# A dilated 3x3 convolution: the last input pair loaded in eighteen transfers instead of one

## The chip, the cores and the metric

The kernel runs on one core of a Trainium2 chip. Five engines take part: TensorE (PE; its weight loads are shown apart as PEld), VectorE (DVE), ScalarE (ACT), GpSimd (POOL) and SyncE (SP), with 16 DMA engines behind the DMA queues. The metric is the device time of one execution in microseconds, as a median of runs. The profile takes one execution apart; its times count from the start of its span.

## The reference

The input holds 16 images of 64 channels, 64 rows and 64 columns, the weights are 128 x 64 x 3 x 3, and the dilation is 2. Each output pixel is a sum over input channels and nine taps that lie two pixels apart, with zeros around the image; all is float32.

```
x_pad = np.pad(x, ((0, 0), (0, 0), (pad, pad), (pad, pad)), mode='constant')
...
output[b, co] += weight[co, ci, kh, kw] * x_pad[b, ci, kh*dilation:kh*dilation+h, kw*dilation:kw*dilation+w]
```

## The kernel before

**Pairs.** Two images of 64 channels fill the 128 partitions, so there are NP = 8 pairs. TensorE works through pair 0 to pair 7. It uses the lower 64 partitions for one image and the upper 64 for the other, with matmuls of the two alternating. Each pair has NU = 4 parts (u = 0 to 3) of 16 rows.

**Arithmetic.** Rows are taken in groups of four, two even ones (e = 0) and two odd ones (e = 1). For the middle tap the kernel first adds the two halves of each group on GpSimd (`prepare`, L127, into s16), convolves that sum once (the "w1" phase), copies the result out of PSUM on ScalarE (L189), and then, for each half, convolves the inputs with differences of weights ("w21", "w01") and with the outer taps, and adds the copied part on VectorE (L194) into the output tile o. So a pair needs both its input x16 and its sums s16.

**Loads.** `load` (L69 to L72) takes a new x16 tile, one of six buffers, and issues from GpSimd's queue a DMA which reads float32 from memory and writes float16 into the tile. Pair 0 is loaded in two transfers, by rows, and pairs 1 to 4 in one each, all at the start. In the loop, at u = 1 of pair pb, the load of pair pb + 2 is put on the queue (L180, L181), for pairs 5, 6 and 7, followed by the first part of the sums of pair pb + 1 (L184) and, at u = 2, by the second (L186). GpSimd takes these in program order, and it runs ahead of TensorE as far as buffers allow: s16 has three buffers, so the sums of pair n wait until TensorE has finished pair n - 3.

**Semaphores.** The completions of the loads on GpSimd's queue go round eight semaphores. In the kernel before there are nine loads, and only the ninth uses a semaphore again, the first one.

**Outputs.** SP issues the output DMAs (L205) when VectorE has filled a tile: two halves of 1 MB in each of two steps for pairs 0 and 7, and two of 2 MB for the others, 20 in all. The output tiles have three buffers.

**Order around the change.** On GpSimd's queue the load of pair 7 comes after the sums of pair 5 and before those of pair 6, which come before those of pair 7. On TensorE, pair 7 first needs its sums (L172 from s16), and then its input (L172 from x16).

Of the kernel before, what the change touches and what calls it, by code (L numbers as in the profile page):

```python
# [10 lines left out]
def kernel(  # L11
# [7 lines left out]
    nc = tc.nc  # L19

    B, CI, H, W = x.shape
# [5 lines left out]
    P = 128  # L27
    f32 = mybir.dt.float32
    f16 = mybir.dt.float16
    NP = B // 2  # L30
# [19 lines left out]
    x16pool = ctx.enter_context(tc.tile_pool(name="x16pool", bufs=6))  # L50
# [8 lines left out]
    x_pair = x.rearrange("(nb two) c h w -> nb (two c) h w", two=2)  # L59
# [5 lines left out]
    x16 = {}  # L65
# [3 lines left out]
    def load(pb, cuts):  # L69
        x16[pb] = x16pool.tile([P, H, W], f16, tag="x16", name=f"x16_{pb}")  # L70
        for lo, hi in zip(cuts, cuts[1:]):
            nc.gpsimd.dma_start(out=x16[pb][:, lo:hi], in_=x_pair[pb, :, lo:hi])  # L72

    cuts0 = [0, 20, 36, 52, H]
    AHEAD = 5
    load(0, [0, 36, H])
    load(1, [0, H])


# [14 lines left out]
    for name, a in (("w21", 2), ("w01", 0)):  # L94
        for u in range(2):
            nc.vector.tensor_sub(  # L96
                out=w16[:, SLOT[name] * KW : (SLOT[name] + 1) * KW, u, :],
# [5 lines left out]
    for n, name in enumerate(("w1", "w21", "w0", "w01", "w2")):  # L103
        ps = cpool.tile([P, 2, NB], f32, tag="ps", name=f"wt{n}")
        k0 = SLOT[name] * KW
        for j in range(KW):
            nc.tensor.matmul(  # L107
                out=ps[:, 0, j * CO : (j + 1) * CO],
# [12 lines left out]
    def prepare(pb, lo, hi):  # L121
        if pb not in s16:
            s16[pb] = sumpool.tile([P, 2 * NQ, W], f16, tag="s16", name=f"s16_{pb}")
        src = x16[pb].rearrange("p (q e r) w -> p q e (r w)", e=2, r=2)
        dst = s16[pb].rearrange("p (q r) w -> p q (r w)", r=2)
        q0, q1 = lo // 4, hi // 4
        nc.gpsimd.tensor_add(  # L127
            out=dst[:, q0:q1], in0=src[:, q0:q1, 0, :], in1=src[:, q0:q1, 1, :]
        )

    prepare(0, 0, 20)
    for pb in range(2, AHEAD):
        load(pb, [0, H])
# [33 lines left out]
    def phase(pb, u, terms):  # L167

        ps = cpool.tile([CO, 2, NB], f32, tag="ps", name="ps")
        for pair in zip(*(conv(pb, hb, ps[:, hb], u, terms) for hb in range(2))):  # L170
            for m in pair:
                nc.tensor.matmul(**m)  # L172
        return ps

    for pb in range(NP):
        o = opool.tile([P, 2, H, W], f32, tag="o", name=f"o{pb}")
        ov = o.rearrange("p b (q e r) w -> p b q e (r w)", e=2, r=2)
        for u in range(NU):

            if u == 1 and AHEAD <= pb + 2 < NP:  # L180
                load(pb + 2, [0, H])  # L181
            if pb + 1 < NP:
                if u == 1:
                    prepare(pb + 1, 0, 36)  # L184
                elif u == 2:
                    prepare(pb + 1, 36, H)  # L186

            s32 = spool.tile([P, 2, NB], f32, tag="s32", name="s32")
            nc.scalar.copy(out=s32, in_=phase(pb, u, [("w1", 2, 0)]))  # L189
            for e, terms in enumerate(  # L190
                ([("w21", 1, 0), ("w0", 1, -1)], [("w01", 0, 0), ("w2", 0, 1)])
            ):
                ps = phase(pb, u, terms)
                nc.vector.tensor_add(  # L194
                    out=ov[:, :, u * UQ : (u + 1) * UQ, e, :],
                    in0=ps.rearrange("p b (q c) -> p b q c", c=QW),
                    in1=s32.rearrange("p b (q c) -> p b q c", c=QW),
                )


            step = NU // 2 if pb in (0, NP - 1) else NU
            if (u + 1) % step == 0:
                fl = slice((u + 1 - step) * 4 * UQ, (u + 1) * 4 * UQ)
                for hb in range(2):
                    nc.sync.dma_start(out=out[2 * pb + hb, :, fl], in_=o[:, hb, fl])  # L205
# [35 lines left out]
```

## Time and profile before

| What | Value |
|---|---|
| Median of 3 runs | 128.02 us (127.53 to 128.8) |
| Profiled execution, its own time | 127.64 us |
| Its span | 125.9 us |
| Granted TensorE clock, mean | 0.956 |
| Matmuls of L172 on x16 | 768, 86.6 us busy |
| Sums on POOL (L127) | 18, 34.0 us busy |
| Loads on POOL's queue (L72) | 9 issues, 570 ns each; to landing 7.1 to 22.8 us |
| Outputs on SP's queue (L205) | 20 issues; to landing 9.1 to 24.9 us |
| Read from and written to memory | 17.07 MB and 33.55 MB |

A page of the profile gives each engine's busy time, then the span in 40 equal slices (a digit is the busy share in tenths), then the DMA queues (q0 is GpSimd's, software_dynamic; q1 is SP's, hardware_dynamic) with the share of the time of 16 DMA engines that their packets took, and the chain of work that ended last. The DMA view gives the same rows of DMA for any stretch of time, with slices of that stretch. A timeline gives an engine's instructions in order: start, duration, line and operation, what it writes and reads, and, in brackets, how long the engine was idle before and what ended that.

### The profile page before, as it was taken

Reading aid. Unit: us, or ns where it says so; the run is one execution under the profiler, and the core shown is the slowest. Engines: PE = TensorE matmul, PEld = TensorE weight load, DVE = VectorE, ACT = ScalarE, POOL = GpSimd, SP = SyncE. Lnnn points to the kernel's source line nnn. Section 1 sums busy time; section 2 is a strip of 40 time slices with the busy share of each in tenths; the row PEclk is TensorE's granted clock in tenths of the full one; section 3 lists DMA queues with packets and bytes.
Section 4 is the critical chain, followed back from the end, with each engine's and each line's share of the span. In section 5 each row is a group of like instructions: output and inputs, shape, how many; then the busy total and the mean of one; then the engine's idle time right before and its main releaser. Section 6 shows DMA issues by size and latency. Waiting matters only on the chain.

```text
span 125.9 us, 2253 instructions
## 1 busy us (share of the span) xinstructions
PE 106.6 (85%) x981; PEld 54.7 (43%) x981; DVE 80.7 (64%) x72; ACT 37.0 (29%) x37; POOL 39.6 (31%) x33
## 2 busy tenths in 40 slices
PE   6348999999999999999999999999999999950000
PEld 2143455555555555555555555555555555520000
DVE  0550367787778777877778778777877787770000
ACT  4733033333333333333333333333333333310000
POOL 6139797868077008600840093000000000000000
PEclk9999999999999999999999999999999999997555
DMA  4899999999999999999999999999999999999981
GB/s 107 143 215 223 213 211 216 234 281 294 401 292 284 383 297 323 328 427 312 312 325 419 427 432 432 437 417 417 437 427 458 417 409 417 437 411 427 427 349 47
DMA packets 4329, 42.37 MB, mean 337 GB/s; under 512 B 480, under 2 KB 480, under 8 KB 864
## 3 DMA queue, kind: packets, MB, share of 16 engines
q1 hardware_dynamic: 3024, 33.85, 63.8%
q0 software_dynamic: 1296, 8.39, 32.9%
q8 instruction: 7, 0.11, 0.3%
q14 instruction: 2, 0.02, 0.0%
HBM read 17.07 MB, written 33.55 MB: 402 GB/s over the span
## 4 chain that ended last, share of the span: by engine, by line
PE 80%; DMA 6%; POOL 1%; DVE 1%; DVEq 1%; issue 1%; POOLq 0%
PE ps L172 80%; DMA x<-in_x_dram 6%; POOL s L127 1%; DVE o L194 1%; DVEq L236 1%; DVEq L194 0%; POOLq L222 0%
## 5 line engine op out<-in xcount | busy, mean ns | idle before, releaser
L194 DVE TENSOR_TENSOR o<-ps,s 128x1024 f32<-128x1024 f32 x64 | 77.0, 1223 | 27.9 <-PE ps L172 26.2
L172 PE MATMUL ps<-x,w_sb 64*128 64x496 f16 (+3 forms) x768 | 86.6, 372 | 0.0
L172 PEld LDWEIGHTS <-w_sb 64*128 64x128 f16 x960 | 52.5, 96 | 51.5 <-issue 5.2
L189 ACT COPY s<-ps 128x1024 f32<-128x1024 f32 x32 | 32.4, 1012 | 70.3 <-PE ps L172 70.3
L127 POOL TENSOR_TENSOR s<-x 128x1152 f16<-128x1152 f16 (+4 forms) x18 | 34.0, 1911 | 36.1 <-PE ps L172 27.8
L172 PE MATMUL ps<-s,w_sb 64*128 64x496 f16 (+1 forms) x192 | 26.5, 379 | 2.1 <-POOL s L127 2.1
L72 POOL DMA_DIRECT2D x<-in_x_dram x9 | 5.1, 570 | 0.8 <-POOLq L222 0.8
L87 PE MATMUL warm<-zero 128*128 128x512 f16 x6 | 2.7, 627 | 1.2 <-DVE zero L81 1.2
L107 PE MATMUL wt<-ident,w 128*128 128x128 f16 x15 | 1.8, 312 | 2.0 <-ACT w L93 2.0
L96 DVE TENSOR_TENSOR w<-w 128x192 f16<-128x192 f32 x4 | 1.7, 495 | 2.5 <-DMA w<-in_weight_dram 2.5
L107 PEld LDWEIGHTS <-w 128*128 128x128 f16 x15 | 1.5, 145 | 2.9 <-ACT w L93 2.9
L93 ACT CAST w<-w 128x576 f16<-128x576 f32 x2 | 2.3, 1212 | 1.6 <-DMA w<-in_weight_dram 1.6
L116 DVE CAST w_sb<-wt 128x384 f16<-128x384 f32 x3 | 1.7, 557 | 1.4 <-PE wt L107 1.2
L87 PEld LDWEIGHTS <-zero 128*128 128x128 f16 x6 | 0.7, 135 | 2.3 <-DVE zero L81 1.2
L93 ACT ACT_TABLE_LOAD x1 | 1.3, 1283 | 0.7 <-PEq L222 0.7
L118 ACT CAST w_sb<-wt 128x384 f16<-128x384 f32 x2 | 1.0, 479 | 1.1 <-PE wt L107 1.1
L81 DVE MEMSET zero<- 128x256 uint32 x1 | 0.3, 272 | 0.9 <-PEq L222 0.9
masks.py:199 POOL TENSOR_SCALAR_AFFINE_SELECT ident<-ident 128x128 f16<-128x128 f16 x1 | 0.3, 295 | 0.1
masks.py:197 POOL MEMSET ident<- 128x128 f16 x1 | 0.2, 233 | 0.0
L222 POOL MEMSET const-float32-0.0<- 128x1 f32 x1 | 0.1, 100 | 0.2 <-issue 0.2
L222 POOL MEMSET const-bfloat16-1.0<- 128x1 bf16 x1 | 0.1, 103 | 0.0
L222 POOL MEMSET const-uint8-127<- 128x1 uint8 x1 | 0.1, 103 | 0.0
(1 smaller groups left out, 0.1 us busy)
## 6 DMA issues: line engine op xcount, KB each, us to landing
out_dram<-o SPq DMA_DIRECT2D x12, 2048.0 KB, 16.8
out_dram<-o SPq DMA_DIRECT2D x8, 1024.0 KB, 12.3
x<-in_x_dram POOLq DMA_DIRECT2D x7, 1024.0 KB, 15.5
x<-in_x_dram POOLq DMA_DIRECT2D x1, 576.0 KB, 7.1
x<-in_x_dram POOLq DMA_DIRECT2D x1, 448.0 KB, 8.6
w<-in_weight_dram SPq DMA_DIRECT2D x1, 288.0 KB, 2.8
```

What stands on the lines that cost most here:

```text
L72: nc.gpsimd.dma_start(out=x16[pb][:, lo:hi], in_=x_pair[pb, :, lo:hi])
L87: nc.tensor.matmul(out=warm[:, 0], lhsT=zero[:, 0:P], rhs=zero, start=True, stop=True)
L93: nc.scalar.copy(out=w16[:, 0:NK, u, :], in_=w32k)
L96: nc.vector.tensor_sub(out=w16[:, SLOT[name] * KW : (SLOT[name] + 1) * KW, u, :], in0=w32k[:, a * KW : (a + 1) * KW, :], in1=w32k[:, KW : ...
L107: nc.tensor.matmul(out=ps[:, 0, j * CO : (j + 1) * CO], lhsT=w16[:, k0 + j, :, :].rearrange("o t i -> o (t i)"), rhs=ident, start=True, st ...
L116: nc.vector.tensor_copy(out=dst, in_=ps[:, 0, 0 : KW * CO])
L118: nc.scalar.copy(out=dst, in_=ps[:, 0, 0 : KW * CO])
L127: nc.gpsimd.tensor_add(out=dst[:, q0:q1], in0=src[:, q0:q1, 0, :], in1=src[:, q0:q1, 1, :])
L172: nc.tensor.matmul(**m)
L189: nc.scalar.copy(out=s32, in_=phase(pb, u, [("w1", 2, 0)]))
L194: nc.vector.tensor_add(out=ov[:, :, u * UQ : (u + 1) * UQ, e, :], in0=ps.rearrange("p b (q c) -> p b q c", c=QW), in1=s32.rearrange("p b ( ...
L236: with _tile.TileContext(nc) as tc:
```

## The change

Pair 7, the last, is no longer loaded by one transfer of 128 partitions with 64 rows, but by 18 transfers, all from GpSimd's queue, at the same place in the program. Partitions 112 to 127 are taken two at a time, eight times: first the rows from 0 to 2, 4, 6 ... 16, another number for each two partitions, and then, in a second round, the rest of their first 20 rows (18, 16, 14 ... 4 rows). Then come rows 20 to 64 of these 16 partitions in one transfer, and at last all rows of partitions 0 to 111 in one. All else stays. As the eight semaphores are used again, GpSimd waits, from the eighth transfer on, for the transfer eight places before (for the eighth, that is the load of pair 6); and TensorE and the sums of pair 7 wait for eight semaphores where they waited for one.

```
+    TWOS = range(P - 16, P, 2)
+    TOP = 20
+
+    def load_twos(pb):
+        x16[pb] = x16pool.tile([P, H, W], f16, tag="x16", name=f"x16_{pb}")
+
+        def part(p0, p1, lo, hi):
+            nc.gpsimd.dma_start(
+                out=x16[pb][p0:p1, lo:hi], in_=x_pair[pb, p0:p1, lo:hi]
+            )
+
+        for n, p in enumerate(TWOS):
+            part(p, p + 2, 0, 2 * n + 2)
+        for n, p in enumerate(TWOS):
+            part(p, p + 2, 2 * n + 2, TOP)
+        part(P - 16, P, TOP, H)
+        part(0, P - 16, 0, H)
...
             if u == 1 and AHEAD <= pb + 2 < NP:
-                load(pb + 2, [0, H])
+                if pb + 2 < NP - 1:
+                    load(pb + 2, [0, H])
+                else:
+                    load_twos(pb + 2)
```

## The prediction

> **What bounds the kernel now.** First I read the page: the row of DMA shares, the queues, and the chain that ended last.
>
> ```profile
> span 125.9 us, 2253 instructions
> ...
> PE 106.6 (85%) x981; PEld 54.7 (43%) x981; DVE 80.7 (64%) x72; ACT 37.0 (29%) x37; POOL 39.6 (31%) x33
> ...
> DMA  4899999999999999999999999999999999999981
> ...
> DMA packets 4329, 42.37 MB, mean 337 GB/s; under 512 B 480, under 2 KB 480, under 8 KB 864
> ...
> q1 hardware_dynamic: 3024, 33.85, 63.8%
> q0 software_dynamic: 1296, 8.39, 32.9%
> ...
> PE 80%; DMA 6%; POOL 1%; DVE 1%; DVEq 1%; issue 1%; POOLq 0%
> ```
>
> The chain names TensorE, but its last piece ends at 113.3 us, 12.6 us before the span does, and the DMA row is at 9 from the third slice nearly to the end. So I asked the DMA view for the stretch after the last load and for the last 6 us.
>
> ```profile
> DMA packets 1771, 22.58 MB, mean 426 GB/s; under 512 B 203, under 2 KB 203, under 8 KB 203
> ...
> q1 hardware_dynamic: 1764, 22.51, 100.0%
> ```
>
> That is 67 to 120 us: the output queue alone fills all 16 DMA engines. The next is 120 to 126 us, in 40 slices of 0.15 us:
>
> ```profile
> DMA  9999999999967671615131312120000000000000
> ```
>
> The engines run dry one after another. The landing records of the last output (sixteen completions, one per engine) run from 121.9 to 124.8 us, with their mean at 123.0. So the end is set by the DMA engine that has most work, not by TensorE: the last two outputs are issued at 113.3 and 113.7 us, and the latest engine comes to them at 119.9 (124.8 less two 1 MB outputs of 2.45 us each, the spacing of the landings at the end). TensorE, VectorE and SP could be about 6 us late before that engine lacked work; only what is added to an engine's packets, or a delay beyond that cover, reaches the end.
>
> Then POOL's timeline, since the change is on its queue:
>
> ```profile
> 51.98 0.57 POOL L72 DMA_DIRECT2D x<-in_x_dram  x1
> 60.20 4.21 POOL L127 TENSOR_TENSOR s<-x 128x1152 f16<-128x1152 f16 x2 [7.65 <-PE ps L172]
> 72.55 4.21 POOL L127 TENSOR_TENSOR s<-x 128x1152 f16<-128x1152 f16 x2 [8.15 <-PE ps L172]
> ```
>
> The first line is the issue of pair 7's load, then the sums of pairs 6 and 7, each waiting for TensorE. POOL does nothing after 76.8. Who needs these? TensorE's timeline:
>
> ```profile
> 96.35 0.81 PE L172 MATMUL ps<-s,w_sb 64*128 64x512 f16 x6
> 96.98 2.55 PE L172 MATMUL ps<-x,w_sb 64*128 64x512 f16 x24
> ```
>
> At 96.35 pair 7 begins with its sums; at 96.98 it reads its input. In time of need the load has 40 us of cover.
>
> **The change part by part.**
>
> *Bytes.* The same elements are loaded once each: 112 full partitions, 16 partitions by 44 rows, and 16 by 20 rows in sixteen pieces. Change in bytes: 0.
>
> *Issues on POOL.* One issue becomes 18. The row of L72 has 0.53 to 0.69 us each; 17 x 0.57 = 9.7 us more on POOL. Behind them stand the sums of pair 6 and then of pair 7.
>
> *New waits on POOL.* Completion semaphores of POOL's loads go round eight, so the eighth small transfer waits for pair 6's load and each later one for the transfer eight before it. Pair 6's load lands at 55.2 (its last completion); the eighth issue comes at 51.98 + 7 x 0.57 = 56.0, so that wait costs nothing. For the others I need a small transfer's round trip, which the trace doesn't show. From below: at least an issue, 0.57 us. From above: a whole load, 15.5 us to landing at this place. I take 5.5: pair 7's load was issued at 51.98 and its first packet after pair 6's stands at 56.49, 4.5 us, and a small piece then takes one turn in its ring and its completion, about 1. So the ninth goes out at 57.5, the seventeenth at about 63.0, the eighteenth (112 partitions) at 63.6. Its data start at 68.1; seven packets per engine, each beside one output packet, are 7 x (0.624 + 0.611) = 8.6 us: landed at about 77, 10 us later than the 67.5 of before. The sum of pair 6 moves from 60.2 to 64.2; TensorE starts that pair near 84.0 (12.4 us before pair 7). The sum of pair 7 starts at 77 for 72.55 and its first part is ready at 79.4; due at 96.35. Both are hidden, by 17 us each; if that cover were gone, TensorE would stall by the excess. Cost: 0.
>
> *What the DMA engines do meanwhile.* While POOL waits, the output queue takes the time: from 52 on it holds 17.8 us of its own packets (its shares from 52 to 75.4, summed), and the next 4 MB come at 63.8. So no engine goes idle, and outputs land earlier while pair 7 lands later. VectorE's only wait for an output (0.69 us at 64.5) can only shrink. Cost: 0.
>
> *Waits on TensorE.* At pair 7 eight semaphores instead of one, spread over a few instructions. All are long complete; some 9 waits at the 17 ns of SP's wait instruction are 0.15 us, under the 6 us of cover. SP's own list is unchanged. Cost: 0.
>
> *Packets on the engines.* This is what reaches the end. Each transfer leaves one 4-byte completion packet on each engine (480 = 30 transfers x 16): 17 more. Their records on the software queue last 9 to 22 ns; 17 x 22 = 0.37 us at most by that row. From above: two 1 MB outputs at the mean spacing of their first landings, 2.49 us each, against one of 2 MB at 4.86 leave 0.12 us per transfer: 17 x 0.12 = 2.0 us. From below: 0, if they fall into gaps. I take 0.37, since it is the duration of the very packet. Two more data packets per engine at 624 - 611 = 13 ns are 0.03. Sum 0.40 us.
>
> *Where the small pieces go.* All sixteen carry 16 x 20 rows of 256 B, 82 KB read. Spread evenly that is 5.1 KB per engine, 0.19 us at 16 KB per 0.611 us. The rows go 2, 4 ... 16 and then 18, 16 ... 4, so if successive transfers go round the engines, every engine gets 20 rows: cost 0. At worst two engines take everything, 41 KB each, 1.53 us: those two end 1.34 us later, the others 0.19 us earlier. No row of this trace has a two-partition transfer; the nearest, the nine loads, put 144 packets each (1296 / 9) over the 16 engines alike, so I take even.
>
> [...]
>
> [...]
>
> *Sum.* The profiled execution took 127.64 us (span 125.9 and 1.74 around it): 127.64 + 0.40 = 128.04. The median of the runs shown is 0.38 above that execution, so the forecast is **128.4 us**.
>
> **The rivals.**
>
> *Each transfer costs what the output spacing allows.* 17 x 0.12 = 2.0 us on every engine, 130.0. For it: it is the difference that the landings show. Against it: the packets themselves last 9 to 22 ns. It passes 1% from 0.075 us each. Chance 0.10.
>
> *The pieces pile up on two engines.* If these are among the last to end, 128.02 + 0.40 + 1.34 = 129.8; if among the first, which have up to 2.9 us to spare, the end moves by 0.40 - 0.19, 128.2. Chance 0.10, half for each.
>
> *The load lands too late.* Place: TensorE's first sum of pair 7 at 96.35. The chain holds two round trips, so the 112 partitions go out at 52 + 2R + 0.6; they must land by 94.0 (2.4 us for the first part of the sum), and from issue to landing they take 13.4 (63.6 to 77), so R must pass 14 us to stall TensorE and about 17 to use up the 6 us as well. At 22.8, the longest landing in the row of L72, the load lands at 112, TensorE is 18 us late and the end 12: 140. For it: loads took 15.5 us to land in this crowd. Against it: most of those 15.5 us are eight packets, not latency. Chance 0.06.
>
> *The latest engines are relieved.* If the small transfers, or the 112 partitions, fall on the engines unevenly and away from the latest ones, the end could come down towards the mean landing, 124.8 to 123.0: -1.8 + 0.4, 126.6. Against it: the even split of every load so far. Chance 0.08.
>
> **How the numbers follow.** The forecast has 0.66, with its own range from 127.6 to 129.0: the packet term from 0 to 0.4 and the runs of before, 127.5 to 128.8. About 1% (1.3 us) is what a measurement of this kernel can tell from no change. Faster by over 1%: the relief, 0.08. Slower: 0.10 + 0.05 + 0.06 = 0.21. The same: 0.66 + 0.05 = 0.71. The range reaches from 127.0 to 130.0; it takes in the piled pieces and the dear completions, and leaves out the late load and most of the relief.
>
> **What would show it.** In the profile after: 18 issues on POOL from about 52 to 64; pair 6's sum at 64 and pair 7's at 77; no wait of TensorE for POOL or for a load near 96; output queue near 100% from 56 to 68 and mixed from 68 to 77; under 512 B 480 + 272 completions; and an end still ragged by about 3 us. It would be wrong if the end moved while TensorE did not, by more than 0.4 us: then packets cost more than they last, or the engines' shares differ; the spread of the last landings tells which. It would be wrong the other way if TensorE waited at 96.

## The result, and the profile after

| | before | changed |
|---|---|---|
| Median of 18 runs | 127.74 us | 128.99 us |
| Ratio | | 1.0082 (95%: 1.0059 to 1.0106) |
| Profiled execution, its span | 127.64, 125.9 us | 129.35, 127.6 us |
| Last output landed: first, mean, last of 16 engines | 121.9, 123.0, 124.8 us | 121.8, 123.4, 126.1 us |
| From the last landing to the end of the execution's time | 2.83 us | 3.29 us |

The kernel became about 1.05 us slower by the ratio, 1.25 us by the medians. A ratio leaves out executions that took over 1.5% more than the fastest of their kernel; a median takes all. The last two rows of the table say where the two profiled executions differ: the mean engine ends 0.4 us later, the latest 1.25 us later, and after that a further 0.46 us passes. (The last row is the execution's own time less the landing, which is counted from the start of the span; about 1.8 us of it lie outside the span in every profile.)

The page of the changed kernel, the rows that answer to those of before:

```profile
span 127.6 us, 2277 instructions
...
PE 106.6 (84%) x981; PEld 54.7 (43%) x981; DVE 80.8 (63%) x72; ACT 37.0 (29%) x37; POOL 48.1 (38%) x50
...
DMA  4999999999999999999999999999999999999950
...
DMA packets 4858, 42.38 MB, mean 332 GB/s; under 512 B 978, under 2 KB 1002, under 8 KB 1408
...
q1 hardware_dynamic: 3024, 33.85, 63.2%
q0 software_dynamic: 1824, 8.39, 32.7%
```

Apart from POOL, which has the 17 further issues, the engines' work is the same, and so are the bytes; the software queue has 528 packets more, nearly all of them tiny, and the DMA engines are as full as before. The DMA view of 120 to 126 us, as before in slices of 0.15 us:

```profile
DMA  6999999999777676723333323121211100101000
```

The first engines run dry where they did, but in this profile the tail is thinner and longer: few engines carry the end. POOL's timeline:

```profile
51.75 3.99 POOL L83 DMA_DIRECT2D x<-in_x_dram  x8
58.25 0.51 POOL L83 DMA_DIRECT2D x<-in_x_dram  x1 [2.50 <-DMA x<-in_x_dram]
59.49 0.50 POOL L83 DMA_DIRECT2D x<-in_x_dram  x1 [0.73 <-DMA x<-in_x_dram]
60.29 0.50 POOL L83 DMA_DIRECT2D x<-in_x_dram  x1 [0.30 <-DMA x<-in_x_dram]
61.48 0.51 POOL L83 DMA_DIRECT2D x<-in_x_dram  x1 [0.69 <-DMA x<-in_x_dram]
...
67.99 0.51 POOL L83 DMA_DIRECT2D x<-in_x_dram  x1 [0.71 <-DMA x<-in_x_dram]
69.22 0.55 POOL L83 DMA_DIRECT2D x<-in_x_dram  x1 [0.72 <-PE ps L192]
69.79 4.22 POOL L147 TENSOR_TENSOR s<-x 128x1152 f16<-128x1152 f16 x2
86.67 4.22 POOL L147 TENSOR_TENSOR s<-x 128x1152 f16<-128x1152 f16 x2 [12.66 <-DMA x<-in_x_dram]
```

Eight issues go out at once, the eighth without a wait, as forecast. From then on one goes out every 1.2 us on average, and the last is issued at 69.2 for the forecast 63.6. Pair 7's sum waits for the load until 86.67. TensorE, for which all this is made:

```profile
96.12 0.81 PE L192 MATMUL ps<-s,w_sb 64*128 64x512 f16 x6
96.76 2.55 PE L192 MATMUL ps<-x,w_sb 64*128 64x512 f16 x24
```

No wait stands in brackets: pair 7 starts at 96.12, even 0.23 us sooner than before. So TensorE lost nothing, and the loss lies behind it.

### The profile page after: what moved, and what is told of

Its sections match the earlier page's. It is cut to its first block, busy times and chain, and to the rows that moved or that the text cites. A ratio compares the mean times of both kernels' runs of the same rounds, so it can differ in the third digit from the quotient of the medians.

```text
span 127.6 us, 2277 instructions
## 1 busy us (share of the span) xinstructions
PE 106.6 (84%) x981; PEld 54.7 (43%) x981; DVE 80.8 (63%) x72; ACT 37.0 (29%) x37; POOL 48.1 (38%) x50
## 4 chain that ended last, share of the span: by engine, by line
PE 79%; DMA 5%; POOL 1%; DVE 1%; DVEq 1%; issue 1%; POOLq 0%
PE ps L192 79%; DMA x<-in_x_dram 5%; POOL s L147 1%; DVE o L217 1%; DVEq L259 1%; DVEq L217 0%; POOLq L245 0%
## 5 line engine op out<-in xcount | busy, mean ns | idle before, releaser
L83 POOL DMA_DIRECT2D x<-in_x_dram x18 | 9.1, 508 | 9.0 <-DMA x<-in_x_dram 8.1
L72 POOL DMA_DIRECT2D x<-in_x_dram x8 | 4.5, 576 | 0.8 <-POOLq L245 0.8
```

The source lines that it names most:

```text
L83: nc.gpsimd.dma_start(out=x16[pb][p0:p1, lo:hi], in_=x_pair[pb, p0:p1, lo:hi])
```

## The experiments

All times are against the kernel before, run beside it on the same chip. The first four ask whether the cost sits in where the small pieces go (theory A) or in each extra transfer, wherever it goes (theory B).

**Even pieces.** The sixteen small transfers take all 16 partitions, two rows each:

```
-        for n, p in enumerate(TWOS):
-            part(p, p + 2, 0, 2 * n + 2)
-        for n, p in enumerate(TWOS):
-            part(p, p + 2, 2 * n + 2, TOP)
+        for n in range(16):
+            part(P - 16, P, 2 * n, 2 * n + 2)
```

(with TOP = 32.) Expected: 

> Same 18 transfers and waits, but the sixteen small ones take all 16 partitions and 2 rows each. Theory A (the pieces of two partitions all fall on the same two DMA engines, and that moves the end): the data are even again, only the completions are left, +0.4 us, ratio near 1.003, mean of the last sixteen landings +0.4 and their spread as in the kernel before, near 2.9 us. Theory B (each extra transfer costs every engine about 0.07 us, wherever its data go): +1.2 us as in the changed kernel, ratio near 1.009.

Measured: 1.0083 (1.0041 to 1.0125), median 128.65 for 127.47. By the time alone, theory A fails. But the profile shows two other things: each of its sixteen pieces per engine is a 512 B read that takes 40 ns where its bytes are worth 19, so by the packet records this kernel pays 0.34 us of its own on every engine (its last landings do not show it: their mean, counted from the landing of an early load, is only 0.26 us above the kernel before); and 3.31 us pass from its last landing to the end, as in the changed kernel and not as in the one before. The experiment did not isolate what it was made for.

**Tall twos.** The second round of two-partition transfers runs to row 64, so the pieces are as heavy as they can be:

```
-            part(p, p + 2, 2 * n + 2, TOP)
-        part(P - 16, P, TOP, H)
+            part(p, p + 2, 2 * n + 2, H)
```

Expected: 

> The twos take all 64 rows of the 16 partitions (no 16-partition transfer), 17 transfers. Theory A: two engines get eight 16 KB reads each, 4.9 us at 0.61, for the one that an even split gives, so +4.3 us there and -0.6 us elsewhere, +0.35 for completions: the end moves by +1.8 (if the two have the spread of 2.9 us to spare) to +4.7 us, ratio 1.014 to 1.037, and the spread of the last landings grows past 5 us. Theory B: 16 extra transfers, +1.1 us, spread unchanged.

Measured: 1.0262 (1.0214 to 1.0309), +3.4 us by the medians. The last output lands on fourteen engines by 125.1 us and on two at 127.2 and 127.7, which is 4.0 and 4.5 us behind the mean of the sixteen; the pieces of two partitions last 5.2 us in all on each of two engines. The DMA view of 120 to 129 us (slices of 0.225 us) shows those two alone at the end: a row of ones, each one engine's packet.

```profile
DMA  9998899763222111210201010101010000000000
```

So the pieces do pile up on two engines. The packet counts show it too. The page's packets under 512 B in the kernel before are 480, 30 transfers by 16 engines. These are the rows of the even pieces and of the tall twos:

```profile
DMA packets 4858, 42.38 MB, mean 334 GB/s; under 512 B 1008, under 2 KB 1008, under 8 KB 1408
```

```profile
DMA packets 4826, 42.38 MB, mean 328 GB/s; under 512 B 962, under 2 KB 974, under 8 KB 1376
```

The even pieces have 480 + 17 x 16 completions + 256 pieces = 1008. The tall twos have 480 + 16 x 16 + 2 pieces = 738, and 224 more: in each of the sixteen two-partition transfers fourteen engines get a 4-byte packet in place of data. The changed kernel's 978 is made in the same way, 480 + 272 + 224 + 2.

**Two parts.** The load only split into 112 and 16 partitions, these in two transfers:

```
-        for n, p in enumerate(TWOS):
-            part(p, p + 2, 0, 2 * n + 2)
-        for n, p in enumerate(TWOS):
-            part(p, p + 2, 2 * n + 2, TOP)
+        part(P - 16, P, 0, TOP)
```

Expected: 

> Three transfers: 16 partitions by 20 rows, the same by 44 rows, and 112 partitions. Theory A: +0.05 us, ratio 1.000 to 1.001. Theory B: two extra transfers, +0.15 us. A third one, that the split into 112 and 16 partitions itself costs (uneven shares of the 112): most of the +1.2 us.

Measured: 1.0004 (0.9971 to 1.0036). The split of 112 and 16 costs nothing that these runs can tell.

**Thirty-four transfers.** In place of all eighteen:

```
+        for n in range(32):
+            part(P - 16, P, 2 * n, 2 * n + 2)
+        part(0, P - 16, 0, 16)
+        part(0, P - 16, 16, H)
```

Expected: 

> 34 transfers, all with even shares: 32 pieces of 16 partitions by 2 rows and the 112 partitions in two. 33 more completions per engine than before. Theory A: 33 x 0.02 = +0.7 us, mean of the last landings +0.7, spread unchanged, ratio near 1.0055. Theory B: 33 x 0.07 = +2.4 us, ratio near 1.019. If the load came too late for TensorE, a wait of TensorE near 96 would show.

Measured: 129.9 to 134.9 us, too uneven for a ratio (1.0214, 1.0144 to 1.0284, rests on two runs). It says nothing on A and B, since it met the rival in which the load lands too late. POOL and then TensorE in its profile, which is of an execution of 132.97 us; the two shortest, 129.92 and 130.53 us, left none:

```profile
84.73 0.54 POOL L83 DMA_DIRECT2D x<-in_x_dram  x1 [0.78 <-DMA x<-in_x_dram]
86.06 0.53 POOL L83 DMA_DIRECT2D x<-in_x_dram  x1 [0.79 <-DMA x<-in_x_dram]
86.60 4.19 POOL L145 TENSOR_TENSOR s<-x 128x1152 f16<-128x1152 f16 x2
105.72 4.19 POOL L145 TENSOR_TENSOR s<-x 128x1152 f16<-128x1152 f16 x2 [14.92 <-DMA x<-in_x_dram]
```

```profile
101.75 2.56 PE L190 MATMUL ps<-x,w_sb 64*128 64x512 f16 x24
108.12 1.35 PE L190 MATMUL ps<-s,w_sb 64*128 64x512 f16 x6 [3.82 <-POOL s L145]
```

Sixteen transfers more hold the last issue back by 17 us, again about 1.1 us each, and TensorE stands still before pair 7.

**What happens after the last landing.** In the profiles the stretch from the last landing to the end is 2.83 us (before), 2.89 (two parts) and 2.88 (thirty-four transfers), but 3.29 (changed), 3.31 (even pieces) and 3.38 (tall twos). SP's waits show where. Each row is who waited for whom: total us, times, longest. Before, then changed:

```profile
SPq L236 <- PEq L236: 0.6, 2, 0.5
```

```profile
SPq L259 <- PEq L259: 1.1, 2, 0.5
```

This is the barrier at the program's end. And the DMA view of the changed kernel's last 1.6 us has one packet:

```profile
DMA packets 1, 0.01 MB, mean 4 GB/s; under 512 B 0, under 2 KB 0, under 8 KB 0
...
q14 instruction: 1, 0.01, 1.7%
```

It is 8 KB of instructions, 0.56 us long, at 127.5, after all outputs; the page's row of this queue counts 2 packets before and 3 here. POOL's program has 54 instructions before, 57 in two parts, 74 or 75 in the kernels with the packet, and 91 in the one with thirty-four transfers (the traces record one fewer of each), where an extra fetch comes at 86 us, in the middle. That gave theory C: POOL's longer program steps into a further 8 KB, and with 74 or 75 instructions it does so only behind the last wait, where nothing hides the fetch.

POOL's instruction records say what the time is lost on. Between its two semaphore instructions in the barrier POOL stands for 0.43 us in the changed kernel, and for 0.06 in the one before. In the tall twos, whose program is one instruction shorter, the pause is 0.41 us and comes one instruction later. The packet starts about 0.7 us after POOL has gone on, within 0.04 us of the span's end. So the loss is a pause of POOL ahead of the packet, and not the time that the packet takes; what POOL does in it the traces do not tell.

**The kernel before, padded.** Nothing but tiny memsets on POOL, of which pad(n) issues n:

```
+    scratch = wpool.tile([P, 1], f16, name="scratch")
...
                 load(pb + 2, [0, H])
+                if pb + 2 == NP - 1:
+                    pad(21)
```

Expected: 

> The kernel before with 21 tiny memsets on POOL behind the load of pair 7, so that POOL's program has as many instructions as the changed kernel's (75 for 54); no transfer is changed. Theory C (about 0.45 us of the cost is a fetch of 8 KB of instructions which POOL's longer program needs only after its last wait, at the very end, so nothing hides it): +0.45 us, ratio 1.0035; the final wait of SP on the barrier near 1.1 us in all for the 0.6 of before; an 8 KB instruction packet after the last output; the landings as before. If the fetch belongs to the transfers: no change, ratio 1.000.

Measured: 1.0078 (1.0033 to 1.0123). The profile has all that theory C asks for (barrier 1.1 us, an 8 KB packet at 125.7, 3.28 us to the end, the landings as before), but the time rose by more than the 0.45 us that it allows, 1.0 us by the ratio and 1.3 by the medians: 7 of 12 runs lay above 128.6, and the profile is of one at 127.5, so it tells nothing of them.

**The changed kernel, padded past the step** (pad(16) behind its transfers). Expected: 

> The changed kernel with 16 more memsets on POOL behind its 18 transfers, so that the step into the next 8 KB of instructions comes in the middle, hidden. Theory C: 0.45 us less than the changed kernel, 128.3 for 128.8, ratio 1.005; barrier wait 0.7; no instruction packet after the last output; the spread of the last landings as in the changed kernel, 3 to 4.3 us. If theory C is wrong: as the changed kernel, ratio 1.008.

Measured: 1.0106 (1.0058 to 1.0153) in six runs. In the profile, which is of the fastest of them, the barrier wait is back at 0.7 and no packet follows the last output (2.88 us to the end), and yet the median was no better than the changed kernel's. Taken by the times, theory C is no better off than its rival here.

**Eight and eight, twelve and four.** These two ask whether the latest engines can be relieved: `part(P - 16, P - 8, 0, H)` and `part(P - 8, P, 0, H)`, or the same cut at 12 and 4. The two-partition transfers had left their data on two engines each, and a packet of a whole partition lasts 0.62 us, so I reckoned that some engines might end about 0.6 us earlier and others as much later. Expected: 

> The last 16 partitions in two transfers of 8 partitions, all rows, and the 112. [...] If shares are dealt in turn: no change, ratio 1.000.

 and 

> The last 16 partitions in transfers of 12 and of 4, all rows, and the 112. [...]

Measured: 1.0033 (1.0009 to 1.0057) and 1.0023 (0.9988 to 1.0059). No relief; the first of the two falls on the side of a small loss. Which engines take these shares and which end last was not found, and no version here beats the kernel before.

**Theory C again, four kernels on one chip.** In the two padded kernels the memsets' tile had been put ahead of others and moved their addresses. Now it lies behind all, and both kernels run at 75 and at 89 instructions:

```
+    padpool = ctx.enter_context(tc.tile_pool(name="padpool", bufs=1))
...
+    scratch = padpool.tile([P, 1], f16, name="scratch")
```

Before with 35 memsets: 

> The kernel before with 35 tiny memsets on POOL behind the load of pair 7 (89 instructions; the memsets' tile lies behind all others, so no address moves). Theory C (the fetch after the last wait costs 0.45 us and only where POOL's program ends just inside a further 8 KB of instructions): the fetch comes in the middle, no change, ratio 1.000, and 2.9 us between the last landing and the end of the time, as before. Theory D (more instructions on POOL disturb the loads of some DMA engine, wherever the fetch lies): as the two padded kernels so far, ratio near 1.008.

Before with 21 memsets: 

> The same with 21 memsets (75 instructions), the padded kernel of before with its addresses left alone. Theory C: +0.45 us, ratio 1.0035, 3.3 us between the last landing and the end. If the shifted addresses made that kernel slow: ratio 1.0035 here against the 1.008 there. Theory D: 1.008 again.

Changed with 16 memsets: 

> The changed kernel with 16 memsets behind its transfers, addresses left alone (89 instructions). Theory C: 0.45 us below the changed kernel of this call, ratio near 1.005; the mean of the last landings 0.4 to 0.5 us above before, counted from the landing of pair 1. Theory D: no gain against it, ratio near 1.009.

Changed, as it is: 

> The changed kernel again, on the chip of the other three: ratio 1.006 to 1.0106 as measured; the fetch after the last landing (3.3 us to the end), the mean of the last landings 0.4 to 0.5 us up, and one or two engines with the small pieces on them, so a spread of 2.7 to 4.3 us.

| POOL instructions | before (127.39 unpadded) | changed |
|---|---|---|
| 89, fetch in the middle | 127.57; 1.0033 (0.9998 to 1.0069) | 128.19; 1.0071 (1.0035 to 1.0107) |
| 75, fetch at the end | 127.87; 1.0031 (1.0001 to 1.0062) | 128.66; 1.0102 (1.0053 to 1.0151) |
| Last landing to the end, 89 and 75 | 2.86 and 3.26 us | 2.90 and 3.30 us |

By the medians, the step from 89 to 75 costs 0.30 us on the one kernel and 0.47 on the other, and in the profiles 0.40 on both. SP's rows of the two padded kernels of before, first 89, then 75:

```profile
SPq L245 <- PEq L245: 0.7, 2, 0.5
```

```profile
SPq L245 <- PEq L245: 1.0, 2, 0.5
```

And their DMA view from just after the last landing to the end, again first 89, then 75:

```profile
DMA packets 0, 0.00 MB, mean 0 GB/s; under 512 B 0, under 2 KB 0, under 8 KB 0
```

```profile
DMA packets 1, 0.01 MB, mean 3 GB/s; under 512 B 0, under 2 KB 0, under 8 KB 0
...
q14 instruction: 1, 0.01, 1.4%
```

Theory C holds: this needs no transfer, only 21 instructions, and 14 more take it away. The ratios alone overlap and would not settle it; the stretch after the last landing does, since it is 2.83 to 2.90 us in eight profiles with 54 to 57 or 89 to 91 instructions, and 3.26 to 3.38 in the six with 74 or 75. POOL's pause in the barrier agrees: 0.06 us in those eight, 0.40 to 0.43 in these six. The first padded kernel's further cost did not come back here; whether the addresses or chance made it was not tried further.

## Why the prediction was right, and where it was not

The forecast was 128.4 us, the same within 1%, in a range from 127.0 to 130.0; 128.99 and 1.0082 lie in it, but the cost was two to three times the 0.40 us of the sum. The range had been made wide for the piled pieces and the dear completions, and neither is what the runs of this kernel show. So that the result lies inside is partly luck, and the interval of the ratio, up to 1.0106, reaches a little past the 1%.

*What bounds the kernel: right.* TensorE was no later, the DMA engines stayed full, and what was added behind them came out at the end.

*Packets on the engines, 0.40 us: right in size, by luck in its parts.* Counted from the landing of an early load (pair 2's; one expectation calls it pair 1's), the mean of the last sixteen landings is 103.7 to 104.0 us in seven profiles without the small pieces, 103.83 on average, and 104.09 to 104.33 in the four of the changed kernel, padded or not, 104.22 on average: +0.39. But I had 17 more packets of 22 ns on each engine. The records of the changed kernel have 31 on average, 17 completions and 14 packets of 4 bytes in place of data, and nearly all last 9 ns: 0.29 us, and 0.03 more for data. The even pieces and the tall twos, with 17 and 16 more completions, are only 0.26 and 0.25 us up, so the term is known to about 0.1 us. The dear completions (0.12 us each) rested on the first landings of each output, which come from the earliest engines; by the means of the sixteen landings two 1 MB outputs take 4.90 to 4.92 us and one of 2 MB, after the loads, 4.87 to 4.99, and no such cost is seen.

*Where the small pieces go, cost 0: the wrong choice.* I took the even split from nine loads that are all 128 partitions wide. In the tall twos the two-partition transfers put all data on the same two engines: two end at 127.2 and 127.7 us, with 5.2 us of pieces on each, and the other fourteen by 125.1. For the changed kernel the packet records give 32 data packets in the software queue, always in two of equal size 0.09 or 0.69 us apart, 1.85 us in all on each of two engines if they are the same two every time, as in the tall twos. Which two they are no run shows. The rival priced this at +1.34 us if the two were among the last engines and -0.19 if among the first. What it cost the changed kernel is not shown. With the fetch equal, the changed kernel is 0.62 us (128.19 - 127.57) and 0.79 us (128.66 - 127.87) above the padded one before; less 0.39 for the mean, 0.2 to 0.4 us are left, but the intervals of these four ratios are 0.4 to 0.6 us to either side, so this rest cannot be told from nothing. The profiles show no longer tail either: the latest landing comes 1.4 to 2.7 us behind the mean, 1.9 on average, in the four of the changed kernel, and 1.5 to 3.4, 2.0 on average, in the seven without the small pieces. And the even pieces, which load all engines alike (256 pieces, no 4-byte packet in place of one), leave as much: 1.06 us by the ratio, less 0.26 for the mean and 0.43 for the fetch, is 0.37. So the two engines are shown, by the tall twos; that they moved this kernel's end is not.

*Issues on POOL, hidden: right in time, wrong in what they bring.* The step that failed outright is that these cost nothing: I costed the 17 issues by their duration and never asked what 21 more instructions do to the program. They put a fetch of 8 KB of instructions behind the last wait, and with it a pause of POOL in the barrier: +0.40 to +0.46 us in the profiles. Where such a packet of 8 KB came in the middle (between 50 and 60 us in the kernel before with 35 memsets), it added nothing behind the last landing: 2.86 us there for the 2.83 of before.

*New waits on POOL: the cover held, the working did not.* I reckoned two round trips of 5.5 us. In fact the pieces pass one after another, 1.2 us each. A transfer leaves on each engine two packets, a data or 4-byte one and the completion (32 data packets, 224 and 256 for the sixteen), and from 56 to 75 us the engines took 525 packets of the software queue and 533 of the output queue, nearly one for one; two output packets of 0.611 us are 1.22. The load landed at 86.4 us for the forecast 77, and the cover for pair 7's first sum shrank to 7 us (ready at 89.1, due at 96.1) where I had given 17. The same pace at thirty-four transfers used it up.

*The sum as it should have been:* 0.39 for packets and 0.43 for the fetch are shown, 0.82 us together, against 1.05 by the ratio (0.75 to 1.35) and 1.25 by the medians. Where the 0.2 to 0.4 us between them come from, if they are there at all, stays open.

## What to carry to other kernels

Here the DMA engines were the bound, and the end was the latest engine's (in the changed kernel the last output landed at 123.4 us on the mean engine and at 126.1 on the latest). So ask of each transfer not only how many bytes it moves but over how many engines; two partitions used two, and with enough bytes on them (the tall twos, 5.2 us on each) these two ended last, at 127.2 and 127.7 us with the others by 125.1. While the output queue took 96.4% of the engines' time (56 to 75 us), a small transfer cost about 1.2 us of lead time, for 0.5 KB as for 4.5: count the transfers against the slack of whoever waits for the last. And look past the last landing: a pause of POOL that came with a fetch of instructions at the very end (0.43 us, for 0.06 before) made up a third or more of this change's cost of 1.05 to 1.25 us, and only the stretch behind the last output shows it.

## What the runs showed that was not expected

A transfer of two partitions left 4-byte packets on the fourteen engines without data, 224 in all. A piece of 512 B read takes 40 ns on its engine for 19 of bytes, and a whole packet of 16 KB read takes 624 for 611, so 13 to 21 ns go with a packet of a load. And one engine can fall behind the others with no more work: in the profile of the even pieces the latest engine alone takes 5.14 us from one 2 MB output to the next between 95 and 111 us, where the others take 4.87, and so ends 1.3 us behind the next. Why is open.
